# A new order of issue for one decoder layer whose instructions stay the same

## The chip, the core and the metric

The kernel runs on one core of a Trainium2 chip. A core has five engines that run side by side, each through its own queue of instructions and in the order of that queue: TensorE (PE) for matmuls, VectorE (DVE), ScalarE (ACT), GpSimd (POOL) and SyncE (SP), whose queue here issues nearly all DMA transfers. They wait for one another by semaphores. The metric is the device time of one launch in microseconds (us); lower is better.

## The reference

It is one layer of a decoder with two token mixers side by side and a gated feed-forward part, for 256 positions, a width of 1024, 8 heads of 128 and an inner width of 2816, all in float32.

```python
h = rmsnorm(x, norm1_g)
u = h @ W_in                                   # rnn_x | rnn_gate | q | k | v | branch gates
A = gelu(rnn_gate) * rg_lru(causal_dwconv4(rnn_x))
B = causal attention(rmsnorm(q), rmsnorm(k), v)  # 256 positions are one block: plain causal
y = sigmoid(g_A) * (A @ P_A) + sigmoid(g_B) * (B @ P_B)
x = x + y @ W_out
h = rmsnorm(x, norm2_g)
x = x + (gelu(causal_dwconv3(h @ W_up)) * (h @ W_gate)) @ W_down
```

## The kernel before

**Precision.** A float32 product is made of three matmuls in a reduced format. A number is split into `hi` (rounded) and `lo` (what is left), and `mm3` adds hi·hi, hi·lo and lo·hi in PSUM. So each weight chunk of 128x2048 arrives in a `raw` buffer (3 of them), ScalarE casts it to `hi` (4 buffers), and VectorE subtracts to get `lo` (3 buffers; `split_part`, line 354). The chunks are numbered in the order in which they are used, 0 to 66: `lo30` is the low half of chunk 30. Activations are split in the same way.

**Stages.** PE goes through k, the recurrent branch with its gates (rx, rg, ri), q, the branch gates ga and gb, v, the attention, the projections pr (P_A) and pa (P_B), wo (W_out), and the feed-forward part: up, gt, dn, and for the gate a form with fewer products whose weights are sums of chunks (`seven`, line 1136: tiles `wq`, `wt`, with halves `hiq`, `loq`, `hit`, `lot`, accumulators `qA`, `qB`, `qC`). The last block of the inner width is handled by itself (`last_up`, `last_gate`, line 1059: `flu`, then `fla`, hi in its first half and lo in its second).

**Attention for a head h** (line 730 on). Scores `s` go to PSUM; VectorE adds the mask and takes the maximum in one instruction per half (`sm`, `mx`), and scales `mx`; ScalarE takes the exponential; VectorE normalises and transposes blocks of 32 into `pd`; two DMAs turn the blocks by way of DRAM (`pm`, and back into `pd`); ScalarE casts `pth`, VectorE makes `ptl`; PE multiplies with v into `o`; ScalarE and VectorE split `o` into `ybh` and `ybl`.

**Ahead of W_out** (lines 823 to 843). The projections are weighted by the gates and summed (`sgb`, from `pa`, `pr` and `sga`). The first half of the channels is transposed by VectorE into `md`, turned by way of DRAM and split into `mh` and `ml`; the second half is transposed on PE (`mT`).

**What sets the order.** The stages' code doesn't issue anything. `Later` (line 213) records each operation: the matmuls in one list, all others in a second one. At the end one call (line 1275) issues them by a table of numbers:

```python
for r in order.split():
    if r[0] == "+":
        ops += [next(pe) for _ in range(int(r))]
    else:
        ops += [self.ops[n] for n in range(int(r.split("-")[0]), int(r.split("-")[-1]) + 1)]
```

A plain number or a span is one or more of the recorded operations; `+n` is the next n matmuls, whose own sequence is fixed. The table thus sets the sequence on VectorE, ScalarE, GpSimd and SyncE, and where each stands between the matmuls. It sets one thing more: a tile gets its buffer only when it is issued, and `Pool.buffer` (line 205) takes the buffer whose last use in the table comes earliest. So a new table also gives other buffers, and with them other waits. Every engine instruction is issued from line 243, which is why all rows of the profile carry that line; the tiles' names tell the groups apart.

Of the kernel before, what the change touches and what calls it, by code (L numbers as in the profile page):

```python
# [119 lines left out]
128-129 +1 146 148 130-131 +1 169 +3 170-171 168 174 205 +1 207 149 132-134 231 150 +4 177 176 199 +6 173 189 +4  # L120
151-158 +1 135-136 175 172 +3 232 +2 139-140 +2 233 +2 234 159-160 235 +1 208 +1 138 137 +3 192 +5 195 +1 200-202 +1
206 182 +1 196-197 +2 183 +1 236-240 +1 178-179 198 180-181 184-185 162 +3 210 212 +3 220 213 +5 327 +2 241-243 +3 161
211 +6 219 244-251 +7 222-223 +3 221 +1 193-194 267 271-272 268-269 275-277 +9 263-265 209 +1 252-254 +3 278 273-274
270 +3 266 +1 255-256 +4 282-283 285 284 257-258 +6 295 279 +2 297 +4 299-300 +6 301 +6 304 +4 280 +1 281 +3 302 316
294 332 +1 298 +1 259 +5 296 +3 260-261 +2 163 165 164 167 166 +4 317 333 303 262 430 +5 330 +6 315 +4 442 +2 431 +4
309 305 +3 310 313-314 311-312 +6 319 337 +2 320 440 307 331 306 308 362-364 366 +2 318 +2 322 +6 321 323 +6 325 340
326 +5 329 +1 360 441 +1 338 432 365 367 +7 324 +6 433 214 286 328 336 +1 218 215 290 217 216 289 288 +1 368-370 +2
371-374 +11 355 341 361 +6 434 +1 375-378 +3 334 +3 335 +3 436 356 443 +3 358 +5 339 287 +1 572 +2 354 291 +10 359 +10
573 588 587 +1 357 +10 344 348 +3 349 351 353 342 346-347 352 392 343 393 350 589 345 391 292 +2 586 449-450 452 +8
451 453-462 +12 435 437 +4 422-423 538 590-591 +10 438 425 402 421 +10 463-465 +2 380 +4 379 381-382 +2 387 389 +1 426  # L130
+11 439 +2 383 394 388 390 395-396 428 398 411 +1 424 +2 384 386 385 480 484 481-482 +3 483 +4 404 403 405-407 +1 412
+18 408-410 +4 413-415 +2 416 397 417 +5 429 +3 489 +1 447 +5 444 +1 418-420 492-494 496 495 506 485 399 401 400 520
+2 445 +2 427 475 523 509 507-508 510 +3 448 +6 505 +7 467 466 468 +5 490-491 +4 446 +3 517 522 521 +1 488 476 487 +1
597 470 469 +3 524 +5 293 +1 474 +2 629 471 473 472 486 618 533 535-536 534 537 +11 498 +5 497 499 +1 515-516 478-479
619 +3 528 477 +1 617 511-514 501 500 518-519 502 504 598 +6 503 559 +14 529-530 526 +1 539 +6 560 563 +2 561-562 +3
547 +1 527 +11 540 531-532 +1 542 +1 525 +4 574 +3 544 +3 548 +2 545 581 +4 550 549 551-553 +8 546 +16 564-566 +1 541
543 +1 554 556 555 575 577 576 578-579 +3 557-558 568 594 567 +7 582 +5 584 +7 592 +1 595 569 571 +1 580 570 601 605
602 596 604 603 +13 607 620 +3 599 608 593 585 621 +6 600 609 615 613 655 610 +8 583 +1 790 +15 616 +2 606 611-612 625
+4 622-623 +8 785 729 614 +10 627-628 +12 631 731-732 +1 626 630 +5 730 787 +5 789 788 624 +7 640 634 641 +10 733 +2
635 +11 632 +1 633 +12 638-639 796 734 +1 644 +10 636 +1 637 +9 646-647 +3 648-650 652 654 651 653 +1 663 +13 645 +7  # L140
797 799 657 +2 786 642 +1 658 664 798 +1 656 670 +1 643 +12 659 +4 662 +7 671 +8 677 +17 660 +1 661 697 +4 667 665-666
668 +6 678 +3 672-673 +10 674-675 +7 698 669 712 +9 801 +1 960 696 676 +1 679 694 680 684 681 683 682 +12 695 800 +2
716 +3 713 +11 699 +1 685 711 702 700-701 +11 717 +1 727 +10 715 +6 686-688 +4 703 689 705 690 692 691 750 +1 724 +2
704 706 708 751 725 748 735 710 709 707 996 714 +2 775 749 +11 736-737 693 738-741 728 742 +11 743-745 765-766 746-747
+2 726 994 +22 776 +1 791 +5 793 +16 721 719-720 718 722 +9 820 +5 998 764 961 774 822 +1 723 752 755 758 761 794 +5
753-754 +5 756-757 792 802 +10 767 +4 759 784 768 826 +2 821 +15 760 999 +4 769 773 770-772 804 +3 837 835 +1 827 823
+10 825 997 +1 839 +3 838 836 +2 841 +6 862 824 +2 840 795 842 803 1005 762-763 +1 995 +21 863 +1 864 +5 813 805 866
+5 861 +1 867 865 +1 875 815 808 877 +11 843 807 811 891 816 806 828 812 814 876 +1 878 844 +11 810 +9 1006 +4 809 926
+1 892 +10 868 817-818 890 +1 869-873 +3 929 829 778 +10 927 +10 930 +1 925 +2 819 777 779 782 955 +6 893 +1 874 783
780-781 928 +2 958 +3 1007 956 +2 954 +15 879-880 1008 883 845 884 +5 962 894 +1 886-888 830 889 959 +4 964 +8 957 +7  # L150
931 +3 932 968 +2 963 1009 +5 965 1010 +12 882 881 832 834 831 885 +5 969 +1 1000 1002 +10 967 966 +1 833 +3 848-849
855 854 846 851 +1 900 +1 857 852 +7 1001 +12 1011 1003 858 +5 1014-1015 +1 850 847 856 853 1016 859-860 916 1018 +5
1013 +14 1023 +8 917-918 993 1017 1019 971 970 +5 1027 1025 +12 919 1024 1022 1021 +5 1004 +1 912 +5 1030 902 910
905-906 904 +2 1026 1028 +9 911 907 901 1032 +1 1031 +10 1012 1029 +1 1020 +4 895 897 +2 898-899 896 +3 933 937 934
936 909 908 903 913 1034 972 935 +3 1033 914 1039 915 +3 1035 +10 1040 1043 +12 920 +2 976 +7 938 +2 1041-1042 +4 1038
973 975 974 +1 1053 1044 +7 1036 1078 1076 1037 1054 921-922 +11 1052 +7 939-940 +5 950-951 923 +1 977 +3 1088 +7 1079
1077 924 +2 1045-1047 1050 1049 1048 +4 1091 947 944 +6 1089 952 945-946 941 948-949 942-943 +8 981 987 +3 1055 +4
1087 982 1056-1057 985 1092 +4 1051 +6 1058 1060 1059 1061 +1 984 +8 1098 953 1099 +5 1101 1094 1093 1095 979 983 980
978 988 1090 +10 1097 +5 1080 1096 1102 1081 +15 986 989-991 1062 +1 1103 +1 1084-1085 1082-1083 +8 1086 1100 +4 1109
# [1179 lines left out]
```

## Time and profile before

| | |
|---|---|
| time, median of 3 runs | 423.8 us (423.72 to 425.75) |
| profiled execution: its own time | 424.38 us |
| profiled execution: span | 422.6 us |
| granted TensorE clock | 1.000 |
| busy share PE / DVE / ACT / POOL | 99% / 85% / 72% / 12% |

The span runs from the first to the last instruction in the trace; the time lies 1.8 us above it. The share of busy time of PE is that of pipelined matmuls with modelled ends, so small waits hide in it: they show in the distance between the starts of neighbouring matmuls.

### The profile page before, as it was taken

The page shows a single profiled execution, that of the slowest core. Times are in us where ns is not written, and L with a number is a line of the kernel's source. Part 1 is how long each engine was busy: PE and PEld are TensorE (multiplying, and loading weights), DVE is VectorE, ACT ScalarE, POOL GpSimd, SP SyncE. Part 2 cuts the span into 40 slices and gives each one's busy share as a digit, 9 for nine tenths or more (in the row PEclk, how much of TensorE's full clock was granted, in tenths as well). Part 3 has the DMA queues.
Part 4 walks back from the last instruction along what each step waited for, and adds up shares of the span by engine and source line. Part 5 has one row for each costly group of instructions (what it writes and reads, how often), then busy time and mean ns, then how long its engine had stood idle before and what let it go on. Part 6 is the DMA issues. An engine that isn't in the chain of part 4 may idle for free.

```text
span 422.6 us, 5428 instructions
## 1 busy us (share of the span) xinstructions
PE 416.9 (99%) x1908; PEld 345.8 (82%) x1908; DVE 359.5 (85%) x439; ACT 304.8 (72%) x381; POOL 51.4 (12%) x101
## 2 busy tenths in 40 slices
PE   8999999999999999999999999999999999999996
PEld 7788888888888887888888888888888888888875
DVE  4769699979899999949999785998999799899953
ACT  3879667899798799686435566569967698897540
POOL 0030788107234000000000000000000000000000
PEclk9999999999999999999999999999999999999999
DMA  7998888499977496899798578583598647779702
GB/s 231 389 388 284 276 258 272 150 342 301 296 291 233 107 325 203 301 339 347 252 314 264 211 244 294 208 297 109 159 338 285 228 158 232 246 265 317 262 2 99
DMA packets 46108, 106.89 MB, mean 253 GB/s; under 512 B 8448, under 2 KB 22656, under 8 KB 43648
## 3 DMA queue, kind: packets, MB, share of 16 engines
...
q10 hardware_dynamic: 720, 0.53, 0.4%
...
q14 instruction: 13, 0.11, 0.1%
HBM read 92.63 MB, written 13.89 MB: 252 GB/s over the span
## 4 chain that ended last, share of the span: by engine, by line
PE 68%; DVE 14%; ACT 11%; issue 3%; DMA 2%; POOL 1%; SPq 1%; DVEq 0%; ACTq 0%
PE acc L243 14%; PE up L243 13%; PE pr L243 5%; PE qA L243 5%; PE wo L243 5%; PE pa L243 5%; PE rx L243 5%; DVE lo L243 5%; PE k L243 4%; ACT hi L243 3%; PE qC L243 3%; PE gt L243 3%; PE last L243 3%; DVE xa L243 2%; ACT L243 2%
## 5 line engine op out<-in xcount | busy, mean ns | idle before, releaser
L243 DVE TENSOR_TENSOR lo<-raw,hi 128x2048 fp32r<-128x2048 f32 (+1 forms) x64 | 141.5, 2215 | 10.1 <-ACT hi L243 7.5
L243 ACT CAST hi<-raw 128x2048 fp32r<-128x2048 f32 (+1 forms) x64 | 118.6, 1857 | 24.7 <-DMA raw<-in_wup 8.1
L243 PE MATMUL up<-lo,h2h 128*128 128x512 f32 x80 | 31.2, 389 | 0.0
L243 PE MATMUL up<-hi,h2h 128*128 128x512 f32 x80 | 31.2, 389 | 0.0
L243 PE MATMUL up<-hi,h2l 128*128 128x512 f32 x80 | 31.1, 389 | 0.0
L243 PE MATMUL acc<-hi,fah 128*128 128x512 f32 x78 | 30.4, 390 | 0.0
L243 PE MATMUL acc<-lo,fah 128*128 128x512 f32 x78 | 30.4, 389 | 0.0
L243 PE MATMUL acc<-hi,fal 128*128 128x512 f32 x78 | 30.4, 389 | 0.0
L243 POOL TENSOR_TENSOR rsq<-rsq 128x8 f32<-128x8 f32 x32 | 21.9, 688 | 37.3 <-DVE rsq L243 35.3
L243 ACT ACT_TABLE_LOAD x14 | 18.0, 1283 | 1.4 <-PEq L1329 1.2
L243 ACT CAST hiq<-wq 128x1024 fp32r<-128x1024 f32 x12 | 12.3, 1048 | 8.2 <-PE up L243 4.0
L243 PEld LDWEIGHTS up<-hi,h2l 128*128 128x128 f32 x80 | 15.0, 188 | 3.1
L243 PEld LDWEIGHTS up<-hi,h2h 128*128 128x128 f32 x80 | 15.0, 188 | 3.1
L243 PEld LDWEIGHTS up<-lo,h2h 128*128 128x128 f32 x80 | 15.0, 188 | 3.1
L243 PEld LDWEIGHTS acc<-hi,fal 128*128 128x128 f32 x78 | 14.6, 188 | 3.1
L243 PEld LDWEIGHTS acc<-hi,fah 128*128 128x128 f32 x78 | 14.6, 188 | 3.1
L243 PEld LDWEIGHTS acc<-lo,fah 128*128 128x128 f32 x78 | 14.6, 188 | 3.1
L243 ACT ACTIVATE fu<-fupd,pv 128x256 f32<-128x256 f32 x32 | 14.8, 504 | 2.6 <-DVE fc L243 2.6
L243 DVE TENSOR_TENSOR loq<-wq,hiq 128x1024 fp32r<-128x1024 f32 x12 | 14.5, 1219 | 2.0 <-PE up L243 1.8
L243 ACT CAST hit<-wq 128x1024 fp32r<-128x1024 f32 x12 | 12.2, 1048 | 5.1 <-PE up L243 5.1
L243 DVE TENSOR_TENSOR wq<-wq,wq 128x1024 f32<-128x1024 f32 x12 | 14.6, 1214 | 0.2
L243 DVE TENSOR_TENSOR lot<-wq,hit 128x1024 fp32r<-128x1024 f32 x12 | 14.1, 1218 | 0.4 <-ACT hit L243 0.4
(302 smaller groups left out, 1169.8 us busy)
## 6 DMA issues: line engine op xcount, KB each, us to landing
...
```

The lines of the kernel that those rows point to most:

```text
L243: getattr(engine, name)(*map(real, a), **{n: real(v) for n, v in k.items()})
```

## The change

The table `ORDER` is replaced by another one. Nothing else differs: the recorded operations, the sequence of the matmuls and the number of buffers are the same. The new table comes from a list schedule and a search over it that use one estimate with longer VectorE and ScalarE instructions. The table is two lines longer, so the issuing line becomes L245. Of its 47 old and 49 new lines two each are enough to see the form:

```diff
@@ -112,53 +112,55 @@
 ORDER = """
-26 0 24 2 4 1 29 +1 31 3 30 32 +1 5 33 +1 6 35 +1 7 37 +1 8 39 +1 9 +3 10-13 +5 15 34 +3 36 +2 14 +4 16 +2 38 +1 40 +2
-41-42 17-18 +5 43-44 +1 47-48 19 +3 45-46 23 +1 49-50 +2 20 224 71 27-28 69 21 70 225-226 51-52 +6 55-56 +4 72 53-54
...
+26 0 4 24-25 1 3 30 32 28 27 2 29 31 +2 5 +1 6 +1 7 +1 8 +1 9 +2 10 +1 11-13 +2 33-34 +3 35-36 15 +5 14 +2 37-38 +2
+39-40 16 +5 41-42 18 +2 43-48 +2 17 +2 19 +3 49 51 50 52 23 +3 20 69 71 +6 55 72 21 +4 53 +2 59 57 +1 56 54 +4 60 22
...
```

ScalarE loads its function table once more (15 instead of 14 times), because the new order changes more often between functions. The rest of the instructions are the same, one for one. Three places follow, as the program orders them (the number behind a tile's name and the underscore only tells tiles of one name apart).

VectorE between the attention's heads, before. `s6` are the scores of head 6, `lo30` belongs to the first chunk of pr:

```order
L243 TENSOR_TENSOR lo29_1610<-raw29_1455,hi29_1587 128x2048
L243 TENSOR_TENSOR ptl2_1627<-pd2_1397,pth2_1625 128x384
L243 TENSOR_TENSOR lo30_1648<-raw30_1484,hi30_1607 128x2048
L243 ISA sm6_1660,mx6_1661<-s6_1650,mask_77 128x256
L243 ISA mx6_1661 128x1
L243 ISA sm6_1660,mx6_1661<-s6_1650,mask_77 128x128
L243 ISA mx6_1661 128x1
L243 SCALAR_TENSOR_TENSOR mx6_1661<-mx6_1661,rq1_1236 128x2
```

The same stretch in the new order:

```order
L245 TENSOR_TENSOR lo29_1601<-raw29_1454,hi29_1570 128x2048
L245 TENSOR_TENSOR ybl0_1591<-o0_1611,ybh0_1587 128x4x2x32
L245 TENSOR_TENSOR ptl2_1622<-pd2_1450,pth2_1620 128x384
L245 ISA sm6_1649,mx6_1650<-s6_1640,mask_77 128x128
L245 ISA mx6_1650 128x1
L245 ISA sm6_1649,mx6_1650<-s6_1640,mask_77 128x256
L245 ISA mx6_1650 128x1
L245 SCALAR_TENSOR_TENSOR mx6_1650<-mx6_1650,rq1_1427 128x2
L245 TENSOR_TENSOR lo30_1675<-raw30_1488,hi30_1598 128x2048
```

`lo30` has moved from ahead of head 6's mask and maximum to behind them, and `ybl0<-o0`, which came six rows behind `mx6`, stands right behind `lo29`.

VectorE at the last block of the inner width, before (`flu` has four rows, of which two are shown):

```order
L243 TENSOR_TENSOR lo64_3536<-raw64_3464,hi64_3511 128x2048
L243 SCALAR_TENSOR_TENSOR flu_3550<-fl1_3546,pv_186,flu_3550 128x255
L243 SCALAR_TENSOR_TENSOR flu_3550<-fl1_3546,pv_186,flu_3550 128x254
...
L243 TENSOR_TENSOR lo65_3571<-raw65_3476,hi65_3534 128x2048
L243 TENSOR_TENSOR flu_3550<-fld_3411,flu_3550 128x2x128 x2
L243 TENSOR_TENSOR fla_3575<-flu_3550,fla_3575 128x512
L243 TENSOR_TENSOR fc4_3394<-gq4_3488,fc4_3394 128x4x128 x2
L243 TENSOR_TENSOR fal4_3598<-fc4_3394,fah4_3596 128x1024
```

The same in the new order:

```order
L245 TENSOR_TENSOR lo63_3510<-raw63_3405,hi63_3457 128x2048
L245 SCALAR_TENSOR_TENSOR flu_3530<-fl1_3520,pv_197,flu_3530 128x255
L245 SCALAR_TENSOR_TENSOR flu_3530<-fl1_3520,pv_197,flu_3530 128x254
...
L245 TENSOR_TENSOR lo64_3556<-raw64_3465,hi64_3527 128x2048
L245 TENSOR_TENSOR flu_3530<-fld_3410,flu_3530 128x2x128 x2
L245 TENSOR_TENSOR fla_3563<-flu_3530,fla_3563 128x512
L245 TENSOR_TENSOR lo65_3576<-raw65_3478,hi65_3549 128x2048
L245 TENSOR_TENSOR fc4_3396<-gq4_3480,fc4_3396 128x4x128 x2
L245 TENSOR_TENSOR fal4_3598<-fc4_3396,fah4_3596 128x1024
```

`lo64` has moved behind the four `flu`, and `lo65` behind `fla`, so that it now stands directly ahead of `fc4` and `fal4`.

ScalarE at head 6, before. `pth6` is the cast of head 6's turned probabilities, `sgb` and `sga` are the branch gates, which get a sigmoid here:

```order
L243 CAST hi32_1740<-raw32_1633 128x2048
L243 CAST ybh0_1583<-o2_1743 128x4x2x32
L243 ACTIVATE sgb1_1781<-gb10_1667,rs1_377 128x512
L243 CAST yah1_1783<-it1_914 128x1024
L243 CAST pth6_1788<-pd6_1710 128x384
L243 ACTIVATE sgb1_1781<-gb11_1671,rs1_377 128x512
L243 CAST ybh1_1805<-o4_1796 128x4x2x32
L243 CAST hi33_1807<-raw33_1678 128x2048
L243 ACT_TABLE_LOAD
L243 ACTIVATE sgb0_1643<-sgb0_1643 128x1024
```

The same in the new order:

```order
L245 CAST hi32_1738<-raw32_1626 128x2048
L245 CAST ybh0_1587<-o2_1742 128x4x2x32
L245 ACT_TABLE_LOAD
L245 ACTIVATE sga1_1379<-sga1_1379 128x1024
L245 ACTIVATE sgb1_1783<-gb10_1653,rs1_385 128x512
L245 ACTIVATE sgb1_1783<-gb11_1661,rs1_385 128x512
L245 CAST hi33_1791<-raw33_1698 128x2048
L245 CAST pth6_1793<-pd6_1715 128x384
L245 ACTIVATE sgb0_1709<-sgb0_1709 128x1024
```

The function table is loaded ahead of `pth6` and not behind it, with the sigmoid of `sga1`; `sgb1<-gb11` and `hi33` have come ahead of `pth6` too. `yah1` has moved up out of this stretch. One more load of the function table, for `sga0`, stands ahead of head 6's exponentials.

Elsewhere: on VectorE, ahead of `md`, two more subtractions of `wq` (`wq010`, `wq000`) and, ahead of `ml0`, `wq001`; on ScalarE the casts `ybh1` of heads 5 and 6 come ahead of `hi34`; on SyncE, the first piece of a weight is loaded ahead of the first piece of x.

More of the change, by code (lines that the diff above doesn't have):

```diff
@@ L114 @@
 ORDER = """
-26 0 24 2 4 1 29 +1 31 3 30 32 +1 5 33 +1 6 35 +1 7 37 +1 8 39 +1 9 +3 10-13 +5 15 34 +3 36 +2 14 +4 16 +2 38 +1 40 +2
-41-42 17-18 +5 43-44 +1 47-48 19 +3 45-46 23 +1 49-50 +2 20 224 71 27-28 69 21 70 225-226 51-52 +6 55-56 +4 72 53-54
-+2 59-60 57 +4 22 +6 61 58 63-66 62 +14 67-68 +13 76-77 +5 74-75 +2 105-106 +3 73 +5 78 +10 108-109 +1 104 +8 102
-79-81 +11 107 82-86 +1 93 142 87 +2 88-92 95 +7 143 +4 187 98 101 99 +2 110 +3 111 +1 94 97 188 141 +16 186 +1 190 96
-227-230 25 +3 117 100 112 114 118 120 115 113 116 +1 103 144 119 121 +4 122-126 +4 204 +5 191 145 147 +1 203 +2 127 +5
@@ L120 @@
[L120 to L159, printed above, removed]
@@ L160 @@
-1104 +8 1064 +1 1063 1065-1067 +2 1068-1071 +11 1110 1072-1075 992 1105 +15 1106-1108 1112 +2 1113 +48 1111 +6
-1114-1115 +3 1116-1117 +3 1118-1119 +5 1120-1121 +1 1122-1123 +5 1124-1125 +1 1126-1127 +6 1128-1129
+26 0 4 24-25 1 3 30 32 28 27 2 29 31 +2 5 +1 6 +1 7 +1 8 +1 9 +2 10 +1 11-13 +2 33-34 +3 35-36 15 +5 14 +2 37-38 +2
+39-40 16 +5 41-42 18 +2 43-48 +2 17 +2 19 +3 49 51 50 52 23 +3 20 69 71 +6 55 72 21 +4 53 +2 59 57 +1 56 54 +4 60 22
++6 63 +3 58 +3 65-66 +1 64 61-62 +3 67-68 +19 76-77 +5 74-75 +2 96 105-106 +4 73 +1 99 +1 102 93 108 78-79 +15 104 +9
@@ new lines @@
+80 109 81-84 +11 107 +1 70 224-226 85-89 +1 90-91 +1 142-143 +7 110 +3 111-112 92 94 +3 95 187-188 +6 141 +5 114 113
++5 98 190 97 117-119 227-228 115-116 +5 186 +3 100 191 +2 204 +2 229 +7 203 +2 121 101 103 144 120 122 230 123 +1
+124-127 +3 145 +3 168 +1 170 205 +10 169 171 174-175 173 189 172 +1 128 +2 129-131 +1 132-133 231 207 +1 146 135 147
++5 232 148 +4 208 134 136 +1 149-153 +9 177 +1 206 +1 176 199-201 195-196 182 +2 233-234 154 235 155-156 +4 140 192
+138 137 139 +1 157-158 236 159 +2 212 178 +1 183-185 +1 210 +4 220 +1 237-238 160 239-240 +3 197 179 198 202 180-181
@@ new lines @@
++1 241-242 +6 222 213 +2 211 223 +5 219 +4 282 +1 221 162 +1 243-246 +10 209 327 +1 193-194 271 263-265 275-278 +2 272
++3 273 266 +1 247 +1 267-268 +1 248-249 +1 283 +7 294-295 285 +2 269 161 270 274 +2 250-254 +2 300 284 +6 302 301 +2
+255-259 +11 297-298 +4 279-280 316 +2 281 +8 299 332 304 +2 296 260-262 +2 317 +10 333 163 315 +5 165 164 166-167 +3
+303 330 +2 309 305-306 +3 307 +6 319-320 331 +6 321 +3 337 +3 324 +6 326 323 +1 308 362-363 329 +5 364-365 310 313-314
+311-312 +1 325 322 +2 430 338 +1 340 +8 318 +2 336 +5 341 431 440 +1 366-371 +9 328 339 +5 214 217 215 218 +5 441 334
@@ new lines @@
++1 372 +2 335 355 +2 373-375 443 286 356 +3 360-361 +7 289 354 287-288 442 432 +3 358 +8 376-378 +4 359 +2 216 +7 290
++1 572-573 589 588 +2 357 +2 342-343 +3 291 +1 348 344-345 433 392 586 +3 349 351-353 350 346 393 +1 347 449 +6 450
+587 452 +3 451 453 +1 454-458 +11 422 434-435 +4 423 +1 391 +7 425 +2 292 402 421 +5 459-463 +7 380 379 381 +1 538 +2
+387 +3 389 +1 426 +11 394-395 436 388 390 +3 424 +5 382-385 +6 386 +2 428 404 +5 403 405-406 480 483 481 484 482 +5
+407 +2 437 396 411 398 +5 408-410 +5 413-416 397 417 +2 429 +8 447 +2 412 399 418 420 401 419 492 427 +1 444 +2 506
@@ new lines @@
+508 510 489 496 494-495 507 493 +1 445 +2 475 +16 467 466 400 +2 464-465 590 468-469 438 +8 448 591 +3 476 520 +2 446
++2 523 522 509 +2 521 524 505 +3 470-471 490-491 472-473 533 +1 478 +5 474 +1 517 +2 293 +5 498 439 487 497 499 +3 500
+511 +4 479 +1 513-514 501 515-516 485 512 488 502 486 503-504 559 +4 536-537 534 +2 535 +2 528 +5 477 +6 597 526 +6
+539 560 +6 529 518 530 519 562 561 +1 547 +1 527 +2 563 +11 540-541 531-532 +2 525 +2 629 +8 574 +3 542 +3 549-550 +1
+581 +2 551-552 +8 553 +1 557 +1 548 +11 564-566 568 618 +2 546 +1 594 +1 554 543 556 +1 544 +1 619 558 555 575 579
@@ new lines @@
+576-578 567 598 +7 620 545 +3 584 +6 569-571 601 +2 592 617 789 603 602 +5 595 +2 582 605 604 +6 596 +2 607 +2 580 +1
+608 615 599 613 655 +12 606 +5 585 621 600 609-610 593 583 +13 616 +6 611-612 622-623 +18 627-628 +13 625-626 630 729
+731 +4 730 +11 614 787 632 788 +5 640-641 +1 732 +8 634-635 +1 733-734 638 +4 790 +19 796 798 639 +1 624 644 785 +14
+800 631 +6 646-647 +3 648-650 +6 636 633 663 637 +11 645 +4 654 653 652 651 +3 658 664 +1 786 670 +3 642 +1 656 659
+643 +1 657 797 799 +15 662 661 +3 671 801 +11 669 +5 677 +6 660 665-666 +2 667-668 +4 697 +3 678 +9 672-673 +4 676 +6
@@ new lines @@
+674-675 +7 698 712 +10 696 +1 679-680 683 682 681 +12 695 702 +1 684-685 +3 713 +12 699 694 700-701 711 +12 716-717
++11 715 +10 686-687 +1 692 748 690 688 703 +2 704 725 724 +1 689 +1 691 706 705 708 710 707 709 714 961 751 765 727 +2
+735 693 736-737 +2 738-741 +3 750 +9 742 728 743-745 960 +1 746-747 +5 766 +1 749 +10 726 997 +13 793 775-776 +6 791
++5 774 764 996 +9 719 718 720-722 +4 792 +6 998 +1 820 +1 723 752 755 758 +3 753 822 +1 784 +1 794 +2 759 +5 756 +2
+803 802 +11 767 +3 821 823 +13 761-762 754 760 768-770 995 771 +11 826-827 +1 835 +4 773 772 +6 825 +1 795 757 +1
@@ new lines @@
+837-838 777 841 839 +3 994 +8 824 862 778 +1 804 +1 842 763 836 840 +13 779 782 999 783 +3 780-781 +3 828 +3 863 +1
+866 864 +10 861 +2 877 808 816 875 829 +9 814 865 1005 867 +2 813 843 +3 845 +1 891 811 805 +1 878 1006 844 876 +11
+812 810 807 +8 926 892 +10 817 +1 890 +1 806 868 1008 869-870 872-873 871 +10 927 +2 848 851 809 815 818 +7 855 854
+849 852 929-930 846 879-880 +1 925 +4 1007 +11 874 955-956 +1 894 +7 819 893 +1 954 883 928 884 882 881 +17 964 958 +3
+886-887 857 962 888-889 959 +2 847 858 856 +5 850 853 +3 957 +7 931 +3 932 +2 968 830 963 1009 833 859-860 +5 885 +20
@@ new lines @@
+969 965 1010 +3 1000 1002 +7 831 834 967 832 900 966 +2 917 +2 916 +8 1001 1011 1003 1012 +11 1018 1014-1015 +10 1016
+918-919 +1 1013 +10 970 +4 1019 1017 1023 +8 971 +3 1024 993 1004 +1 1027 1025 +10 907 912 +1 1022 1021 +5 903 910 906
+901 909 904 +6 905 +1 1028 1026 +1 1030 +8 911 908 +1 895-896 898-899 897 +2 1020 +4 1031 +2 1034 +7 902 913-914 +1
+1029 +4 933 936 934 937 935 +6 1032-1033 +1 1039 +4 1035 +2 920 +6 1043 915 +2 1040 +11 1038 +3 938 +2 972 974-976 973
++5 1041-1042 +1 1053 +9 922 +2 1036 1078 1076 +1 921 1054 +10 1037 1044 1052 +3 923 +2 939-940 947 +7 950 944 977 +1
@@ new lines @@
+1077 +1 1088 +4 1079 +5 951 +2 1045 948-949 +1 1046 1050 1047 1049 1048 +3 941 +2 1091 +4 1089 945-946 952 +4 989 +6
+982 987 986 +1 1055 924 +1 1087 +2 1056-1058 1061 1059 984 +5 1060 +5 1092 942-943 +2 1098 985 978 953 981 +5 1051 +1
+1080 +7 988 979 1101 +3 1099 +1 1090 +7 1062 +3 1097 1081 1083-1085 1082 1086 +10 1093-1096 980 983 990-991 +2 1102 +8
+1064 +5 1103 1063 1065-1067 +4 1068-1071 +7 1109 +5 1104 +3 1072-1075 +10 1110 +5 1100 +8 992 1106 1105 1107-1108 +5
+1112-1113 +45 1111 +6 1114-1115 +5 1116-1117 +1 1118-1119 +3 1120-1121 +5 1122-1123 +3 1124-1125 +1 1126 +6 1128 1127
@@ L162 @@
+1129
 """
```

## The prediction

> **What bounds the kernel now.** The page of the profiled execution comes first, since its first lines say which engine the time belongs to.
>
> ```profile
> span 422.6 us, 5428 instructions
> PE 416.9 (99%) x1908; PEld 345.8 (82%) x1908; DVE 359.5 (85%) x439; ACT 304.8 (72%) x381; POOL 51.4 (12%) x101
> PEclk9999999999999999999999999999999999999999
> ...
> L243 ACT ACT_TABLE_LOAD x14 | 18.0, 1283 | 1.4 <-PEq L1329 1.2
> ...
> L243 DVE TENSOR_TENSOR wq<-wq,wq 128x1024 f32<-128x1024 f32 x12 | 14.6, 1214 | 0.2
> ```
>
> TensorE (PE) is busy for 416.9 of 422.6 us at its full clock. A change in the order of issue alone takes no matmul away, so it can win only what PE spends waiting, and it can lose whatever it makes PE wait for. So the next view is the list of PE's waits, and behind it the chain of work that ended last, for the pace of a stretch in which PE never waits.
>
> ```profile
> PE k L243 <- ACT his L243: 0.8, 2, 0.4
> PE o L243 <- DVE mx L243: 0.4, 1, 0.4
> PE k L243 <- DVE his L243: 0.3, 1, 0.3
> ...
> 380.83 37.16 PE acc L243 x162
> ```
>
> The two waits of `k` (1.1 us together) belong to the first 12 us. After that only one wait is named in the whole run, the one of `o` for VectorE (DVE). A wait can also be smeared over several matmuls, and then no row names it. I therefore looked for stretches where the starts of neighbouring 128x512 matmuls lie further apart than usual. The usual step follows from the chain: 162 matmuls in 37.16 us are 0.229 us each, and that stretch holds the one slow place below; without its 0.36 us and the last matmul's tail the step is 0.227 us. Two places stand out in PE's timeline.
>
> ```profile
> 168.52 0.39 PE L243 MATMUL gb<-hi,xgl 128*128 128x512 f32 x1
> 169.35 0.36 PE L243 MATMUL o<-pth,vh 128*128 128x256 f32 x1 [0.44 <-DVE mx L243]
> ...
> 402.24 0.39 PE L243 MATMUL acc<-hi,fal 128*128 128x512 f32 x1
> 402.46 0.46 PE L243 MATMUL acc<-hi,fla 128*128 128x512 f32 x1
> 402.76 0.39 PE L243 MATMUL acc<-lo,fla 128*128 128x512 f32 x1
> 403.15 0.74 PE L243 MATMUL acc<-hi,fla 128*128 128x512 f32 x2
> 403.73 0.40 PE L243 MATMUL acc<-lo,fla 128*128 128x512 f32 x1
> ```
>
> At the first, 0.83 us lie between two starts instead of 0.227: **0.60 us** are lost, a little more than the 0.44 us of the wait itself. At the second, five steps take 1.49 us instead of 1.135: **0.36 us** are lost. Together 0.96 us, or 0.2% of the run, is all that PE loses after the start. That is the ceiling of what this change can win there.
>
> **The change part by part.** It removes and adds no arithmetic. Every matmul keeps its place among the matmuls, and the other instructions are the same ones, except for one more load of ScalarE's (ACT's) function table, 15 instead of 14. So each term is a matter of what is queued ahead of an instruction that PE waits for.
>
> *VectorE at heads 6 and 7.* The first matmul of `o` for head 2 needs the PSUM bank of the scores `s6`, which comes free when `sm6`/`mx6` have been read.
>
> ```profile
> 165.90 0.55 DVE L243 TENSOR_TENSOR ptl<-pd,pth 128x384 fp32r<-128x384 f32 x1
> 166.36 2.29 DVE L243 TENSOR_TENSOR lo<-raw,hi 128x2048 fp32r<-128x2048 f32 x1
> 168.57 0.42 DVE L243 CUSTOM_DVE_ANT_0 sm<-s,mask 128x256 f32<-128x256 f32 x1
> 169.24 0.16 DVE L243 SCALAR_TENSOR_TENSOR mx<-mx,rq 128x2 f32<-128x2 f32 x1
> ```
>
> `lo30` holds VectorE from 166.36 to 168.57 and the mask of head 6 comes only then. In the new order the mask stands ahead of `lo30`: it moves up by 2.2 us, less the `ybl0<-o0` that is put ahead of it (about 0.34 us of pitch). The two scores parts are then read by about 167.5, and the matmul wants to start at 168.75. The bank that `o` takes may change with the order; the other candidate, that of `o0`, is read still earlier. Term: **-0.60 us**. If something else on VectorE runs up to 1.2 us later, the cover still holds; if it is gone, the old 0.60 returns, which bounds this term by -0.60 and 0.
>
> *VectorE at the last part of the FFN.* `fla` is the last activation block. Its chain runs `flu` (VectorE), a gelu (ACT), the product with the gate (VectorE), `fla` hi (ACT), `fla` lo (VectorE).
>
> ```profile
> 395.51 0.59 ACT L243 ACTIVATE flu<-fl,pv 128x256 f32<-128x256 f32 x1
> ...
> 396.87 1.91 DVE L243 SCALAR_TENSOR_TENSOR flu<-fl,pv,flu 128x255 f32<-128x255 f32 x4
> 398.70 2.28 DVE L243 TENSOR_TENSOR lo<-raw,hi 128x2048 fp32r<-128x2048 f32 x1
> 400.90 0.75 DVE L243 TENSOR_TENSOR flu<-fld,flu 128x256 f32<-128x256 f32 x2
> 402.40 0.69 DVE L243 TENSOR_TENSOR fla<-flu,fla 128x512 fp32r<-128x512 f32 x1 [0.74 <-ACT fla L243]
> 403.36 1.29 DVE L243 TENSOR_TENSOR fc<-gq,fc 128x512 f32<-128x512 f32 x2 [0.27 <-ACT fc L243]
> ```
>
> Now `lo65` (398.70 to 400.90) goes behind `fla`, and `lo64` goes between the four `flu` and the product. The four `flu` can begin when ACT has delivered, at 396.10, and take 1.83 us of pitch, to 397.93. `lo64` takes 2.20 us like `lo65`, to 400.13. From the product's start to the start of `fla` lo are 1.50 us (402.40 - 400.90), so `fla` lo starts at 401.63 instead of 402.40 and everything for it is 0.77 us earlier. The loss was 0.36. Term: **-0.36 us**, bounded by 0, because PE itself arrives up to 0.60 us earlier if the first wait is gone, and then 0.77 covers only 0.17 of the 0.36 unless VectorE's stream moves up with PE.
>
> *What is late next.* `lo65` now stands ahead of `fc4` and `fal4`.
>
> ```profile
> 405.82 1.23 DVE L243 TENSOR_TENSOR fal<-fc,fah 128x1024 fp32r<-128x1024 f32 x1 [1.17 <-ACT fah L243]
> ...
> 408.76 0.39 PE L243 MATMUL acc<-hi,fal 128*128 128x512 f32 x1
> ```
>
> After `fla` lo ends at 402.32, `lo65` takes VectorE to 404.5, where `fc4` began at 403.36 before. So `fal4` ends 1.14 us later, at 408.19 instead of 407.05. PE uses it at 408.76, or at 407.80 once the 0.96 us are won. If VectorE's stream stays where it is, PE waits 0.39 us here; if it moves up with PE, nothing. A second estimate agrees in size: in the old order some 16 producers stand at most one matmul ahead of their user, and two of them cost 0.96 us; the new order has some 12 such places, which at the same rate make 0.72 us. The true cost lies between 0 and 0.72; I take the value next to the row of `fal4`: **+0.36 us**.
>
> *ScalarE at head 6.* Ahead of `pth6` the new order has 5.06 us more work: two table loads, the evacuation `sgb1<-gb11` (0.58 us) and the cast `hi33` (1.92 us).
>
> ```profile
> 180.83 0.51 ACT L243 CAST pth<-pd 128x384 fp32r<-128x384 f32 x1 [4.74 <-DMA pd<-pm]
> ...
> 184.02 1.28 ACT L243 ACT_TABLE_LOAD   x1
> 185.31 2.01 ACT L243 ACTIVATE sgb<-sgb 128x1024 f32<-128x1024 f32 x2
> ...
> 181.38 0.56 DVE L243 TENSOR_TENSOR ptl<-pd,pth 128x384 fp32r<-128x384 f32 x1 [1.27 <-ACT pth L243]
> ...
> 183.94 0.28 PE L243 MATMUL o<-ptl,vh 128*128 128x256 f32 x1
> ```
>
> The cover is the idle time of 4.74 us in which ACT waited for the transposed `pd6`. So 5.06 us make `pth6` 0.32 us late, and `ptl6`, which ended at 181.94 for a use at 183.94, has 2.00 us to give. Term: **0**, with 1.7 us to spare. If the cover is gone, 5.06 - 2.00 = 3.06 us are lost. The table loads I cost by their row, 1.28 us each: behind the one at 184.02 the next activation starts at 185.31, at once, and the idle time ahead of all 14 is 1.4 us, of which 1.2 is at the start.
>
> The Trainium skill, in "ScalarE: Activation LUTs", section "What ACT_TABLE_LOAD costs", adds a drain of some 1380 ns to those 1283 ns for every switch. The trace agrees on the 1283 and shows no drain beside it. By that rule `pth6` would be another 2.76 us late, and as an estimate from that page 1.1 us would be added to the sum; I go by the rows.
>
> *VectorE ahead of W_out.* Two more 128x1024 subtractions of `wq` stand ahead of the transposition `md`, and the pair `wq001` ahead of `ml0`, 2.3 to 2.4 us more in all at 1.21 us each.
>
> ```profile
> 184.03 2.29 DVE L243 TENSOR_TENSOR lo<-raw,hi 128x2048 fp32r<-128x2048 f32 x1 [1.38 <-ACT hi L243]
> 188.72 0.56 DVE L243 TENSOR_TENSOR ptl<-pd,pth 128x384 fp32r<-128x384 f32 x1 [2.39 <-ACT pth L243]
> 190.79 0.76 DVE L243 TENSOR_TENSOR ybl<-o,ybh 128x256 fp32r<-128x256 f32 x2 [1.52 <-ACT ybh L243]
> ...
> 219.38 1.23 DVE L243 TENSOR_TENSOR ml<-md,mh 128x1024 fp32r<-128x1024 f32 x1 [0.23 <-ACT mh L243]
> ...
> 221.08 0.39 PE L243 MATMUL wo<-hi,ml 128*128 128x512 f32 x1
> ```
>
> `ml0` ends at 220.61 and is used at 221.08: 0.47 us to spare, and 0.23 of idle time just ahead of it. The rest of the 2.4 us must come out of the idle time from 182 to 191, 1.38 + 2.39 + 1.52 = 5.29 us. It can, since the new order also brings `pth7` and the `ybh` casts in front of `hi34`, so that VectorE gets on sooner. Term: **0**; without the cover 2.4 - 0.47 - 0.23 = 1.7 us.
>
> *The start.* The first piece of a weight and the first piece of x change places among the loads. The same pieces are there ahead of the load for which `k` waits longest, so I cost it at **0**, bounded by the 1.1 us of the two rows of `k` on the side of a gain and by about 0.3 us (one wait of that kind) on the other.
>
> **The sum**, against the profiled execution's own 424.38 us, which is 0.58 above the median of 423.8: 424.38 - 0.60 - 0.36 + 0.36 = 423.78 us, which is **423.2 us** when brought to the median.
>
> **The rivals.** Half a per cent, 2.1 us, is about what a measurement of this kernel can tell from no change.
>
> *A, the forecast, 0.46.* Both waits go, and up to 0.8 us returns at other places: 422.8 to 423.6, likeliest 423.2.
>
> *B, the waits only move, 0.22.* An order found by an estimate needn't keep what it promises: PE loses about 0.96 us again, at `fal4` and at other tight places, and the run takes 423.8 us. For it speaks that VectorE has little room: it is busy for 85% of the run. Against it, 12 tight places are fewer than 16.
>
> *C, ACT comes late to head 6, 0.17.* This is the rival on the other side. Its place is `pth6`; it decides from the point at which ACT comes to `hi32` more than 1.7 us later than now. For it speaks that `pth6` now has two more table loads ahead of it than before; against it, that the 4.74 us of idle time stand in the row. At its full price 424.38 - 0.96 + 3.06 = 426.48, or 425.9 by the median; half of it gives 424.4. PE has no gap over 0.6 us behind the start, and its clock is full. The Trainium skill, in "TensorE: Matmul & The Clock Gate", section "HAM oscillation — how this bites in real kernels", says that a gap of more than some 3.4 us lets the clock drop; no run here shows that, and it would only make C dearer.
>
> *D, VectorE comes late to W_out, 0.11.* The place is `ml0`, with the 1.7 us above: 424.38 - 0.96 + 1.7 = 425.1, or 424.5 by the median. It decides if less than 1.7 us of the idle time from 182 to 191 is really used.
>
> *E, the start shortens as well, 0.04.* The two waits of `k` go and nothing returns: 424.38 - 0.96 - 1.1 = 422.3, or 421.7 by the median.
>
> **How the numbers follow.** The range runs from 422.4 to 426.0 us: it leaves out E below and the part of C beyond its full price above, with some mishaps together, in all less than 2 in 10. The forecast's own range is 422.8 to 423.6. Faster by over 0.5% means under 421.7: most of E, 0.03. Slower by over 0.5% means over 425.9: 0.11 out of C, 0.03 out of D with a second wait beside it, 0.04 for several waits like those of B that add up; 0.18. The rest, 0.79, is no change that can be told.
>
> **What would show it.** In the list of waits of the changed kernel the row of `o` for `mx` should be gone, and the matmuls of `fla` should start 0.23 us apart. The first `o<-pth` of head 6 and the first `wo<-hi,ml` should follow their neighbours without a gap; a wait there for ACT `pth` or DVE `ml` is C or D. A gap at `acc<-hi,fal` behind the `fla` block, about 0.4 us, is the term that I put at +0.36. The pace of the first 12 us should be the old one. I'm wrong if PE waits at a place that I haven't named for more than 0.7 us in all, or if the span falls by more than 1.5 us.

## The result

The new order is slower: 429.25 us against 424.12 us for the old one, a ratio of 1.0115 with a 95% interval of 1.0081 to 1.0149. The forecast was 423.2 us, at most 426.0. The two waits that it expected to go did go; what it didn't have are two new ones, earlier in the program, and a drop of the clock behind them.

The page of the new order, and its list of PE's waits behind the start:

```profile
span 427.3 us, 5450 instructions
PE 418.9 (98%) x1908; PEld 348.4 (82%) x1908; DVE 359.5 (84%) x439; ACT 305.7 (72%) x382; POOL 52.3 (12%) x101
PEclk9999999999999899999999999999999999999999
```

```profile
PE s L245 <- DVE qTl L245: 2.3, 1, 2.3
PE ga L245 <- DVE lo L245: 1.8, 1, 1.8
```

VectorE's busy time is that of before to the tenth (359.5 us), and ScalarE's grew by 0.9 us, less than one table load. So the time did not go into work. Neither of the two rows stood in the old list, and the row of `o` for `mx` is gone. In PE's timeline the two places look like this, with what follows the second one:

```profile
121.50 0.47 PE L245 MATMUL ga<-hi,xgh 128*128 128x512 f32 x1
123.80 0.50 PE L245 MATMUL ga<-lo,xgh 128*128 128x512 f32 x1 [1.83 <-DVE lo L245]
...
139.53 0.28 PE L245 MATMUL s<-kTl,qTh 128*128 128x128 f32 x1
142.14 0.33 PE L245 MATMUL s<-kTh,qTl 128*128 128x128 f32 x1 [2.34 <-DVE qTl L245]
...
143.67 0.63 PE L245 MATMUL v<-lo,xgh 128*128 128x512 f32 x1
...
146.23 0.63 PE L245 MATMUL v<-lo,xgh 128*128 128x512 f32 x1
146.66 0.56 PE L245 MATMUL v<-hi,xgl 128*128 128x512 f32 x1
147.05 0.40 PE L245 MATMUL v<-hi,xgh 128*128 128x512 f32 x1
```

The first gap is 2.30 us from start to start instead of 0.227, the second 2.61 instead of 0.11. Behind the second, eight matmuls from 143.67 to 147.05 start 0.42 us apart instead of 0.227 and last 0.63 us instead of 0.39; the row `PEclk` has its only 8 there. And the places that the forecast named:

```profile
174.24 0.39 PE L245 MATMUL gb<-hi,xgl 128*128 128x512 f32 x1
174.47 0.28 PE L245 MATMUL o<-pth,vh 128*128 128x256 f32 x1
...
407.76 0.39 PE L245 MATMUL acc<-lo,fla 128*128 128x512 f32 x1
407.99 0.61 PE L245 MATMUL acc<-hi,fla 128*128 128x512 f32 x2
```

`o` follows `gb` after 0.23 us (0.83 before), and the matmuls of `fla` start 0.23 us apart. Since the matmuls come in the same sequence in both kernels, each one's start can be set against its own start before, and the lag of the new order grows or shrinks only where something happens. From the start of the span to the last matmul, which starts at 419.14 before and at 423.81 now:

| place | lag gained, us |
|---|---|
| the first 14 us | -0.46 |
| `ga` for `lo22` | +2.20 |
| `s` for `qTl1` | +2.55 |
| eight matmuls at half pace | +1.59 |
| `o` for `mx6`, and the matmul behind it | -0.68 |
| `fla` | -0.38 |
| all else | -0.16 |
| sum | +4.66 |

The span grew by as much, 427.3 - 422.6 = 4.7 us.

### The profile page after: what moved, and what is told of

Its sections match the earlier page's. It is cut to its first block, busy times and chain, and to the rows that moved or that the text cites. A ratio compares the mean times of both kernels' runs of the same rounds, so it can differ in the third digit from the quotient of the medians.

```text
span 427.3 us, 5450 instructions
## 1 busy us (share of the span) xinstructions
PE 418.9 (98%) x1908; PEld 348.4 (82%) x1908; DVE 359.5 (84%) x439; ACT 305.7 (72%) x382; POOL 52.3 (12%) x101
## 4 chain that ended last, share of the span: by engine, by line
PE 84%; DVE 7%; issue 3%; ACT 2%; DMA 1%; POOL 1%; SPq 0%; DVEq 0%; ACTq 0%
PE acc L245 14%; PE up L245 13%; PE k L245 5%; PE pr L245 5%; PE gb L245 5%; PE qA L245 5%; PE wo L245 5%; PE pa L245 5%; PE rg L245 5%; PE rx L245 5%; PE qC L245 3%; PE gt L245 3%; PE last L245 3%; PE v L245 2%; DVE lo L245 2%
## 5 line engine op out<-in xcount | busy, mean ns | idle before, releaser
L245 DVE TENSOR_TENSOR lo<-raw,hi 128x2048 fp32r<-128x2048 f32 (+1 forms) x64 | 141.7, 2217 | 19.3 <-ACT hi L245 16.1
L245 ACT CAST hi<-raw 128x2048 fp32r<-128x2048 f32 (+1 forms) x64 | 118.4, 1856 | 26.0 <-DMA raw<-in_wpa 6.8
L245 PE MATMUL up<-hi,h2l 128*128 128x512 f32 x80 | 31.1, 389 | 0.0
L245 PE MATMUL up<-hi,h2h 128*128 128x512 f32 x80 | 31.1, 389 | 0.0
L245 PE MATMUL up<-lo,h2h 128*128 128x512 f32 x80 | 31.1, 389 | 0.0
L245 PE MATMUL acc<-lo,fah 128*128 128x512 f32 x78 | 30.4, 390 | 0.0
L245 PE MATMUL acc<-hi,fah 128*128 128x512 f32 x78 | 30.4, 390 | 0.0
L245 PE MATMUL acc<-hi,fal 128*128 128x512 f32 x78 | 30.4, 389 | 0.0
L245 POOL TENSOR_TENSOR rsq<-rsq 128x8 f32<-128x8 f32 x32 | 21.0, 658 | 36.4 <-DVE rsq L245 34.3
L245 PEld LDWEIGHTS up<-lo,h2h 128*128 128x128 f32 x80 | 15.0, 188 | 3.1
L245 PEld LDWEIGHTS up<-hi,h2l 128*128 128x128 f32 x80 | 15.0, 188 | 3.1
L245 PEld LDWEIGHTS up<-hi,h2h 128*128 128x128 f32 x80 | 15.0, 188 | 3.1
L245 PEld LDWEIGHTS acc<-hi,fal 128*128 128x128 f32 x78 | 14.6, 188 | 3.1
L245 PEld LDWEIGHTS acc<-hi,fah 128*128 128x128 f32 x78 | 14.6, 188 | 3.1
L245 PEld LDWEIGHTS acc<-lo,fah 128*128 128x128 f32 x78 | 14.6, 188 | 3.1
L245 DVE TENSOR_TENSOR loq<-wq,hiq 128x1024 fp32r<-128x1024 f32 x12 | 14.5, 1216 | 2.4 <-ACT fu L245 1.4
L245 DVE TENSOR_TENSOR lot<-wq,hit 128x1024 fp32r<-128x1024 f32 x12 | 14.4, 1219 | 2.2 <-PE last L245 1.6
L245 ACT ACTIVATE fu<-fupd,pv 128x256 f32<-128x256 f32 x32 | 14.7, 498 | 1.3 <-DVE fal L245 1.3
L245 DVE TENSOR_TENSOR wq<-wq,wq 128x1024 f32<-128x1024 f32 x12 | 14.5, 1219 | 0.2
L245 PE MATMUL ga<-lo,xgh 128*128 128x512 f32 x32 | 12.6, 394 | 1.8 <-DVE lo L245 1.8
L245 ACT CAST hit<-wq 128x1024 fp32r<-128x1024 f32 x12 | 12.3, 1049 | 2.6 <-DVE wq L245 1.7
```

The costliest lines, as they stand in the source:

```text
L245: getattr(engine, name)(*map(real, a), **{n: real(v) for n, v in k.items()})
```

## The experiments

Two trails lead back from the two waits. The first, on ScalarE, in the old order and then in the new one:

```profile
111.58 0.67 ACT L243 ACTIVATE sqq<-q,rs 128x512 f32<-128x512 f32 x1
112.14 1.05 ACT L243 ACTIVATE qTh<-qd 128x1024 fp32r<-128x1024 f32 x1
115.47 0.69 ACT L243 ACTIVATE sqq<-q,rs 128x512 f32<-128x512 f32 x1 [2.28 <-DVE qd L243]
116.06 1.90 ACT L243 CAST hi<-raw 128x2048 fp32r<-128x2048 f32 x1
```

```profile
109.48 1.04 ACT L245 ACTIVATE qTh<-qd 128x1024 fp32r<-128x1024 f32 x1
116.56 0.69 ACT L245 ACTIVATE sqq<-q,rs 128x512 f32<-128x512 f32 x1 [6.04 <-DVE qd L245]
117.27 1.28 ACT L245 ACT_TABLE_LOAD   x1
118.56 1.06 ACT L245 ACTIVATE tt<-rt 128x1024 f32<-128x1024 f32 x1
119.53 1.89 ACT L245 CAST hi<-raw 128x2048 fp32r<-128x2048 f32 x1
```

ScalarE stands idle for 6.04 us ahead of `sqq10`, the square of a half of q. ScalarE's square and VectorE's transposition `qd1<-q10` both read the same PSUM bank, and the program lets two engines read one bank only one behind the other, in the order of the table. In the old table the square came first and VectorE waited for it (it was long done). In the new table the transposition comes first, and VectorE reaches it late, so ScalarE waits, and with it everything queued behind: the table load, `tt1`, and the cast `hi22`, which is 3.5 us later than before. `lo22` starts at 121.45, and the matmul wanted it at 121.73.

The second trail, on VectorE, old and new:

```profile
135.37 1.23 DVE L243 TENSOR_TENSOR qTl<-qd,qTh 128x1024 fp32r<-128x1024 f32 x1
...
138.41 2.29 DVE L243 TENSOR_TENSOR lo<-raw,hi 128x2048 fp32r<-128x2048 f32 x1
```

```profile
138.66 2.29 DVE L245 TENSOR_TENSOR lo<-raw,hi 128x2048 fp32r<-128x2048 f32 x1
140.87 1.22 DVE L245 TENSOR_TENSOR qTl<-qd,qTh 128x1024 fp32r<-128x1024 f32 x1
```

`lo25` now stands ahead of `qTl1`. The theory: the turned wait, the place of `qTl1`, and a clock that follows the gaps make up the loss. The rival: VectorE is late as a whole. All kernels below are one of the two orders with one to four numbers of the table moved; the numbers are those of the operations, and the arithmetic is the same everywhere. Each diff shows only the parts of the table's lines that change. By the table's rule for buffers, none of the moves in the new order changes the buffer of any tile, so buffers have no part in what those moves win back.

**The square first** (344 is `sqq10`, 348 the transposition `qd1<-q10`):

```diff
- +1 348 344-345 433 392 586
+ +1 344 348 345 433 392 586
```

> The new order with one instruction moved: ScalarE's square of q10 (sqq10) is issued ahead of VectorE's transposition of the same PSUM bank (qd1<-q10), as in the old order. Theory (the new order costs 2.2 us at the ga matmul because ScalarE, 6.0 us idle behind that transposition, casts hi22 late; 2.5 us at the s matmul because qTl1 stands behind lo25; 1.6 us by eight matmuls at half clock that follow these two waits): the 6.0 us of ScalarE's idle time and the wait of ga for lo go, 2.2 us; the wait of s for qTl stays between 1.5 and 3 us, since VectorE and PE both come 2.2 us earlier. 427.0 us, or 425.5 if the half clock needs both waits. Rival (VectorE is late from 4 us of idle time that the new order leaves it between 12 and 80 us, and both waits come from that): the wait of ga stays above 1.5 us and the time within 1 us of the new order's.

Measured: 424.54 us, 1.0010 of the old order (1.0001 to 1.0018), 4.7 us less than the new order. On ScalarE and PE:

```profile
111.36 0.67 ACT L245 ACTIVATE sqq<-q,rs 128x512 f32<-128x512 f32 x1
...
114.31 1.89 ACT L245 CAST hi<-raw 128x2048 fp32r<-128x2048 f32 x1
...
139.32 0.33 PE L245 MATMUL s<-kTh,qTl 128*128 128x128 f32 x1 [1.49 <-DVE qTl L245]
```

One number moved by one place, and `hi22` is 5.2 us earlier, the wait of `ga` is gone, that for `qTl` has shrunk to a loss of 1.65 us, and behind it no matmul runs at half pace. The time fell further than either figure of the theory: the wait for `qTl` was partly a consequence of the first one, and the clock stayed up (0.999 or 1.000 in all 11 executions).

**The cast first** (392 is `hi22`): the square keeps its wait, but the cast no longer stands behind it.

```diff
- +1 348 344-345 433 392 586
+ +1 348 392 344-345 433 586
```

> The new order with the cast hi22 ahead of the square sqq10 on ScalarE; the square still waits for VectorE's transposition. Theory: it is not the square's wait as such but the cast queued behind it that PE feels, so the wait of ga goes here too, while ScalarE still idles 4 us or more ahead of sqq10: 427.0 us (425.5 if the half clock needs both waits), within 0.7 us of the kernel with the square first. Rival (the work behind sqq10, tt1 and rt1, is what becomes late): the wait of ga goes but another of 1 us or more takes its place.

Measured: 427.01 us, 1.0072 (1.0048 to 1.0095).

```profile
111.64 1.89 ACT L245 CAST hi<-raw 128x2048 fp32r<-128x2048 f32 x1
117.45 0.69 ACT L245 ACTIVATE sqq<-q,rs 128x512 f32<-128x512 f32 x1 [3.92 <-DVE qd L245]
...
141.22 0.47 PE L245 MATMUL s<-kTh,qTl 128*128 128x128 f32 x1 [2.91 <-DVE qTl L245]
...
142.24 0.63 PE L245 MATMUL v<-hi,xgh 128*128 128x512 f32 x1
...
146.93 0.61 PE L245 MATMUL v<-hi,xgl 128*128 128x512 f32 x1
147.36 0.42 PE L245 MATMUL v<-hi,xgh 128*128 128x512 f32 x1
```

The loss at `ga` falls to 0.5 us, so it was the cast behind the square that PE felt. But the square and what follows stay late, and the loss at `qTl` grows to 3.1 us, with half pace up to 147.36. Here the rival (something behind the square becomes late in its turn) was right, and the kernel is 2.5 us slower than the one with the square first. The profile shows the slowest of its six executions, 429.33 us; the clock stayed up in two of the others, which took 425.70 and 426.00 us.

**`qTl1` first** (412 is `qTl1`, 429 `lo25`):

```diff
- 417 +2 429 +8 447 +2 412 399
+ 417 +2 412 429 +8 447 +2 399
```

> The new order with qTl1 ahead of lo25 on VectorE. Theory: the wait of s for qTl (2.5 us) goes or falls below 0.5 us, since lo25 holds VectorE for 2.2 us; the wait of ga (2.2 us) stays. 425.1 us if the half clock follows the longer gap, 426.7 if the gap at ga alone brings it about. Rival (VectorE is late anyway): 0.3 us or more of the wait remains and lo25, now 1.1 us later, makes v wait: no gain above 1.5 us.

Measured: 426.83 us, 1.0062 (1.0048 to 1.0076).

```profile
PE ga L245 <- DVE lo L245: 1.8, 1, 1.8
...
PE o L245 <- ACT pth L245: 0.8, 1, 0.8
```

The loss at `qTl` falls from 2.5 to 0.3 us. That at `ga` stays, 0.5 us ahead of one matmul and 2.2 ahead of the next, and in this profile all matmuls behind them keep the full pace. A new loss of 1.5 us appears behind them, at the first `o` that needs `pth0`. The time is near the 426.7 us of the theory, but by luck: that figure counted on half pace behind `ga`, where the profile has the new loss instead. Two of the five executions had a mean clock of 0.996 (426.68 and 426.98 us), so the clock can drop in this kernel as well.

**Both moves:**

```diff
- +1 348 344-345 433 392 586
+ +1 344 348 345 433 392 586
- 417 +2 429 +8 447 +2 412 399
+ 417 +2 412 429 +8 447 +2 399
```

> The new order with both moves (square first, qTl1 ahead of lo25). Theory: both waits and the half clock go, 6.2 us; what is left against the old order are the gains at the start (0.4 us), at o (0.6) and at fla (0.3): 422.8 us, 1.3 us below the old order. Rival (the estimate behind the new order leaves VectorE late as a whole): other waits of 1 us or more in all appear behind the two, 424 us or more.

Measured: 423.93 us, 0.9998 (0.9989 to 1.0006). Both waits and the half pace are gone, but the gains don't show, since a wait has come up in the attention, 0.96 us in all:

```profile
PE o L245 <- ACT pth L245: 0.3, 1, 0.3
...
PE o L245 <- DVE ptl L245: 0.2, 1, 0.2
```

So the rival was half right: behind the large waits a smaller one was hidden. The next three kernels follow it. (515 is `pth0`, 511 and 513 are the two evacuations `vh1` on ScalarE; 516 is `ptl0`, 514 and 512 are the two `vl1` on VectorE, 485 is a scan.)

**`pth0` ahead of `vh1`**, with both moves above:

```diff
- 511 +4 479 +1 513-514 501 515-516 485 512
+ 515 511 +4 479 +1 513-514 501 516 485 512
```

> The new order with three moves: square first, qTl1 ahead of lo25, and ScalarE's pth0 ahead of the two evacuations vh1. With the first two moves alone a wait of 0.96 us is left, that of o for pth0 and ptl0. Theory (that wait alone eats the gains at o, fla and the start): it goes, as pth0 comes about 1.2 us earlier, and the time is 423.0 us, 0.9 to 1.0 below the old order. Rival (VectorE and ScalarE are late as a whole in the attention, so each repair shows the next wait): another wait of 0.5 us or more comes at o or at v, and the time stays at 423.9.

Measured: 423.71 us, 0.9997 (0.9989 to 1.0006). `pth0` now comes 1.7 us earlier, but VectorE makes its low half behind a `vl1`, ahead of which it waits 1.2 us for ScalarE's `vh1`, and 1.15 us are lost at the matmul that needs it. The rival was right:

```profile
156.03 0.75 DVE L245 SCALAR_TENSOR_TENSOR vl<-v,rs,vh 128x512 fp32r<-128x512 f32 x1 [1.20 <-ACT vh L245]
156.69 0.55 DVE L245 TENSOR_TENSOR ptl<-pd,pth 128x384 fp32r<-128x384 f32 x1
```

**`ptl0` ahead of one `vl1`**, against the kernel before:

```diff
- 513-514 501 516 485 512
+ 513-514 501 485 516 512
```

> The new order with four moves: the three before and, on VectorE, ptl0 ahead of vl1, whose cast now comes after pth0. Theory (after the third move the wait of o for pth0 went, but ptl0 stood behind vl1, which waits 1.2 us for ScalarE): ptl0 ends at 155.5 us instead of 157.2 and is used at 156.3, so the last wait of 1.15 us goes; 422.7 us, 1.1 us below the old order. Rival (the next wait shows up in its place): 0.5 us or more at another matmul, 423.4 us or more.

Measured: 424.45 us, 1.0015 (1.0000 to 1.0030). The move was mistaken: of the two `vl1`, 512 is the later one, so `ptl0` came behind the scan as well, and the loss grew from 1.15 to 1.51 us.

**`ptl0` ahead of both**, against the kernel with `pth0` ahead of `vh1`:

```diff
- 513-514 501 516 485 512
+ 513 516 514 501 485 512
```

> The new order with square first, qTl1 ahead of lo25, pth0 ahead of vh1 and, this time, ptl0 ahead of the first of the two vl1 (the move before had put it behind a scan, 0.6 us later, and the wait grew by 0.36 us). Theory: ptl0 no longer stands behind the 1.2 us in which VectorE waits for vh1, ends at about 155.4 us and is used at 156.2: the wait goes, 422.7 to 423.0 us, the same as the old order with two moves. Rival (the next tight place): 0.5 us or more at another matmul, 423.4 us or more.

Measured: 422.80 us, 0.9978 (0.9968 to 0.9988). The wait of `o` is gone. What is left behind the start is one wait, and 0.5 us lost by it:

```profile
PE pr L245 <- DVE yal L245: 0.4, 1, 0.4
```

So the new order with four numbers moved is some 6 us faster than the new order (422.80 us against 429.25, from different rounds) and 1.0 us faster than the old one.

**The same places in the old order.** First `qTl1` behind `lo25` alone:

```diff
- 405-407 +1 412 +18 408-410
- 417 +5 429 +3
+ 405-407 +19 408-410
+ 417 +5 429 412 +3
```

> The old order with qTl1 behind lo25, where the new order has it. Theory (the place of qTl1 costs by itself): lo25 ends at 140.6 us as before, qTl1 at 141.8 instead of 136.6, its matmul wants it at 137.9: a wait of 3.5 to 4 us, and behind it matmuls at half clock as in the new order, 1.5 to 3 us; 429 to 431 us. Rival (the wait for qTl is made by a late VectorE and not by the place): below 1 us, 424 to 425 us, all at full clock.

Measured: 429.11 us, 1.0127 (1.0112 to 1.0142).

```profile
137.82 2.29 DVE L243 TENSOR_TENSOR lo<-raw,hi 128x2048 fp32r<-128x2048 f32 x1
140.03 1.22 DVE L243 TENSOR_TENSOR qTl<-qd,qTh 128x1024 fp32r<-128x1024 f32 x1
...
141.30 0.42 PE L243 MATMUL s<-kTh,qTl 128*128 128x128 f32 x1 [3.82 <-DVE qTl L243]
...
142.26 0.63 PE L243 MATMUL v<-hi,xgh 128*128 128x512 f32 x1
...
144.82 0.40 PE L243 MATMUL v<-hi,xgh 128*128 128x512 f32 x1
```

A VectorE that is not late at all loses 4.0 us here, and the half pace follows. The place of `qTl1` costs by itself; the rival of a late VectorE falls for this wait. (This move, and that of the short gap below, also change the buffers of some tiles, but only of tiles issued behind the wait.)

Then the turned square alone:

```diff
- 344 348
+ 348 344
```

> The old order with the square sqq10 issued behind VectorE's transposition of the same bank, as in the new order. Theory (the turned wait does its harm only together with what stands between the square and hi22 in the new order, a table load and tt1, 2.3 us): ScalarE idles some 2 us longer ahead of sqq10, lo22 is ready about 0.9 us later and still 1 us ahead of its use: within 0.4 us of the old order, no wait of ga. Rival (the turned wait alone is enough): ga waits 1.5 us or more, 425.5 us or above.

Measured: 424.79 us, 1.0029 (1.0018 to 1.0041). ScalarE idles 3.2 us ahead of the first square instead of 2.3 us ahead of the second, and `ga` doesn't wait:

```profile
114.33 0.69 ACT L243 ACTIVATE sqq<-q,rs 128x512 f32<-128x512 f32 x1 [3.21 <-DVE qd L243]
```

So the turned wait alone isn't enough for the loss at `ga`. What else it takes was not separated: in the new order a table load and `tt1` stand between the square and the cast, and VectorE also comes 1.7 us later to the transposition. But the turned wait isn't free, which I had expected within 0.4 us: 0.95 us are lost, in its profile 0.37 at `v` and 0.55 at `s` for `ybl`.

A shorter gap, made by `qTl1` behind `mx0` and one product of `it0`:

```diff
- 538 590-591
- 405-407 +1 412 +18 408-410 +4 413-415 +2
+ 538 591
+ 405-407 +19 408-410 +4 413-415 590 412 +2
```

> The old order with qTl1 and one product of it0 (0.6 us) behind mx0 and ahead of lo25. qTl1 would end at 140.2 us for a use at 137.9: one gap of 2.3 us on PE, with no other gap near it. If the half clock needs a gap of 2.4 us or more, or a second gap 18 us before as in the new order, all matmuls behind stay at full clock and the time is 426.1 us; if a gap of 2.3 us is enough, 8 to 15 matmuls follow at 0.43 us apart and the time is 427.5 us or more.

Measured: 425.37 us, 1.0032 (1.0018 to 1.0046).

```profile
PE s L243 <- DVE qTl L243: 1.6, 1, 1.6
```

The gap came out at 1.76 us of loss, not 2.3, with all matmuls behind it at full pace. It says nothing on 2.3 us.

Last, the two gains alone, in the old order (548 is `lo30`, 1110 is `lo65`):

```diff
- +3 544 +3 548 +2 545 581 +4 550 549 551-553
- +11 1110 1072-1075 992
+ +3 544 +5 545 581 +4 550 549 551 548 552-553
+ +11 1072-1075 1110 992
```

> The old order with two moves taken from the new one: lo30 behind mx6 and lo65 behind fla. Theory (the two slow places of the old order are worth 0.60 and 0.36 us by themselves): 423.0 us, 0.9 to 1.0 below the old order, no row of o for mx, and fla at its usual pace. Rival (what is won at o is lost again at the next tight place): less than 0.4 us below the old order.

> The old order with lo30 behind mx6 and lo65 behind fla once more, on the same chip as the repaired new order. If both orders then hold no wait behind the start, they agree within 0.4 us, at 422.7 to 423.1 us; if the new order's remaining differences are worth something, the repaired new order is 0.5 us or more faster.

Measured: 423.00 us, 0.9978 (0.9969 to 0.9988), and the second time 422.93 us, 0.9969 (0.9955 to 0.9982). PE's list has no wait behind the start, and at `fla`, the second time:

```profile
401.24 0.39 PE L243 MATMUL acc<-hi,fla 128*128 128x512 f32 x1
401.46 0.39 PE L243 MATMUL acc<-lo,fla 128*128 128x512 f32 x1
401.69 0.62 PE L243 MATMUL acc<-hi,fla 128*128 128x512 f32 x2
```

Beside the old order's profile PE gains 0.60 us at `o`, 0.08 at the matmul behind it and 0.37 at `fla`, and nothing is lost behind it. The second time it ran beside the kernel with `ptl0` behind the scan, which still had its 1.5 us, so the comparison of two orders without waits, for which it was meant, has to go by the ratios to the old order: the repaired new order lies 0.22% below the old order, and this one 0.22% and 0.31%. That is no difference that the runs can tell.

## Why the prediction was wrong

**What bounds the kernel** was right. PE is full, and the ceiling of 0.96 us for what can be won is about what the two moves alone bring: 0.84 and 1.23 us in two comparisons.

**The two terms of the gain** were right in sign and size: -0.60 us at `o` was forecast and measured (0.68 with the matmul behind it), -0.36 us at `fla` was forecast and 0.37 to 0.38 measured, in the new order and in the old one with the two moves.

**ScalarE at head 6, VectorE ahead of W_out, the start.** All three were put at 0. No wait of `o` for `pth6` and none of `wo` for `ml` stands in the new order's list. That is weak evidence, as PE came there 5 us late; the stronger one is the repaired order, in which PE is some 0.4 us ahead of the old one at these places and has no such wait either. The start did vary by up to 0.8 us, but as much among kernels that share one order of loads as between the two orders; the swap shows no effect of its own. Rivals C and D did not happen.

**What is late next** is the step that failed. The prediction put all new waits at 0.36 us, between 0 and 0.72, partly from the row of `fal4` and partly from a count of places where a producer stands at most one matmul ahead of its user. `fal4` cost nothing: VectorE's stream moved up with PE. The count was no bound. The two waits that came cost 2.2 and 2.5 us, the half pace behind them 1.6 us, and neither place is in the count. `qTl1` stands 18 matmuls ahead of its user (55 before). They take 3.8 us, and `lo25` and `qTl1` together only 3.4 us, but VectorE came to `lo25` at 138.66, 0.98 us before PE wanted the result. `lo22` was late because of an instruction two engines away. What tells such a place is not how far ahead the producer stands in the table but when its engine gets to it. The prediction's own sign of being wrong, more than 0.7 us of waits at places that it hadn't named, is what happened.

**The idle time was taken as cover.** Extra work ahead of an instruction was set against the idle time that the old profile shows ahead of it. That holds only as long as the idle time has the same cause. In the new order the square waits for the transposition, where before the transposition waited for the square, and ScalarE's 6 us of idle time lie behind VectorE's queue. The list of instructions shows the two rows in both orders; that the wait had turned shows only in which of the two comes first, and in the trace as the 6.04 us ahead of the square. The prediction looked at the order from head 6 on and not at this stretch.

**The rivals.** The forecast had a rival of the right kind (a queue that comes late and makes PE wait, 425.9 us at its full price) at the wrong place, and too cheap: it priced one wait, where two came and the clock went down behind them. Rival B (the waits only move) is what is left after two repairs, 423.93 us.

**The clock** was set aside, as no gap over 0.6 us stood in the old profile. In the profile the 1.6 us of matmuls at half pace are a third of the loss. That they come with the gaps is borne out by the counts of the last section: the mean clock fell in five of the new order's six executions and in none of the old order's 81 beside the experiments. The prediction cited the Trainium skill, "TensorE: Matmul & The Clock Gate", section "HAM oscillation — how this bites in real kernels", for a limit of some 3.4 us. Here a gap of 2.5 us, with one of 2.2 us 18 us before it, was enough, so by the measurement the term belongs to rivals with smaller gaps than that too.
